# A long causal convolution: the layout in DRAM of a tile's rows, and the transfers that read four shifted copies of it back

## The chip, the cores and the metric

One core of one Trainium2 chip runs the whole program in one launch. The metric is the time of one execution on the device, in microseconds (us); the kernel before takes 1078.66 us in the median of three runs. Names of engines: PE is TensorE (matmuls), DVE is VectorE, ACT is ScalarE, POOL is GpSimd, SP is SyncE, which here only issues transfers.

## The reference

A small model in float32 on 256 positions of width 1024: a block with sliding-window attention and an mLSTM, cross attention, a gated feed-forward; then a conformer convolution module, a second feed-forward, a sparse attention, a third feed-forward. The change touches the convolution module alone, which is:

```
def conformer_conv_module(h, w_in, b_in, w_dw, b_dw, ln_g, ln_b, w_out):
    a, g = jnp.split(h @ w_in + b_in, 2, axis=-1)
    u = a * jax.nn.sigmoid(g)
    u = lax.conv_general_dilated(
        u, w_dw[:, None, :].astype(u.dtype), window_strides=(1,),
        padding=[(CONV_WIDTH - 1, 0)], dimension_numbers=('NWC', 'WIO', 'NWC'),
        feature_group_count=D_MODEL) + b_dw
    ...
    uf = (uf - mu) * lax.rsqrt(var + LN_EPS) * ln_g.astype(jnp.float32) + ln_b.astype(jnp.float32)
    u = jax.nn.silu(uf).astype(h.dtype)
    return u @ w_out
```

`CONV_WIDTH` is 31 and the convolution is depthwise: each of the 1024 channels has 31 taps of its own over time, and sees only earlier positions. `mu` and `var` are mean and variance over the channels of one position.

## The kernel before

Activations lie with channels on the 128 partitions and time along the row: a tensor of 1024 channels is 8 tiles m = 0 to 7 of 128 x 256. Weights stream from DRAM in 512 KB pieces (`wraw`, issued by SP, four buffers) and most are split by ACT and DVE into a high and a low half (`wpr`), so that three fast matmuls make one float32 product (L260 to L262).

The convolution module is the function `conformer`. For each tile m it has these steps, named as in the code:

- `p` (PE, L1120): the product with `w_in`; `g`, `h` (DVE, ACT): scaling and the gate; `u` (DVE, L1143): the gated tile, written into `uz`, where 19 zero columns stand before its 256 columns. A row of `uz` has ZW = 275 numbers, 1100 bytes.
- `w` (POOL, L1150): a transfer of the tile to DRAM, into one of five buffers `cz`, row p of the tile as row p of the buffer.
- `c` (POOL, L1158): four transfers back into SBUF, into one of five buffers `crp`. Copy s (0 to 3) is shifted by s columns and goes to partitions 32 s to 32 s + 31; on partition 32 s + c lie the channels c, 32 + c, 64 + c and 96 + c, each as a piece of 272 numbers (1088 bytes). For tiles 5 to 7 the step first loads the tile's tap weights (`cwd`, L1077), which for tiles 0 to 4 are loaded at the stage's start.
- `t` (PE, L1167): 16 or 20 tap matmuls (the profile counts each of them twice). Since a partition group holds the same 32 channels at four shifts, one matmul with a sparse weight of 128 x 32 does four taps of 32 channels. The first 16 or 20 of the 31 taps of a tile are done so.
- `d`, `v`, `n`, `y` (DVE, ACT, L1197 and near): the other taps, one multiply-add over the tile each; `m` (DVE, L1210): the sum of both parts; `q`, `s` (ACT, PE, L1243): sums for the layer norm. After tile 7's sums come mean, variance and the product with `w_out` (steps `sf` to `o`), one after the other.

The order of the steps on each engine is worked out when the program is built. `Plan.run` simulates the engines with the time that each step is given (`step(name, engine, us, need, rank, lag=...)`: `us` is how long it holds its engine, `lag` how much later its result is there) and issues the steps in the order of their planned starts. Each engine then works its queue strictly in that order; what really releases a step are semaphores. A transfer issued by POOL signals one of eight semaphores in turn, and an issue waits until the transfer eight places before has landed. POOL has little other work in this stage than `w`, `c` and the loads of taps. In the profile a transfer issued by POOL shows as POOL's instruction DMA_DIRECT2D for its issue; its landing is told by "DMA cz<-cuz" or "DMA crp<-cz" as the releaser of a wait.

Of the kernel before, what the change touches and what calls it, by code (L numbers as in the profile page):

```python
# [132 lines left out]
class Net:  # L133
# [919 lines left out]
    def conformer(self, first, pool):  # L1053
        nc = self.nc
        W = 31
        PAD = 4 * max(CONV_G) - 4
        ZW = PAD + 3 + S
        NREP = 5
        uz = pool.tile([P, KT, ZW], F32, name="cuz")
# [3 lines left out]
        zs = [dram.tile([P, ZW], F32, name=f"cz{i}")[:, :] for i in range(NREP)]  # L1063
# [11 lines left out]
        def taps_of(m):  # L1075
            wd[m] = pool.tile([P, max(CONV_G), P], F32, name="cwd", tag="cwd", bufs=NREP)
            nc.gpsimd.dma_start(wd[m][:, 0 : CONV_G[m]], self.T["c_dw"][:, m, 0 : CONV_G[m], :])  # L1077
# [18 lines left out]
        def step(name, eng, us, need=(), rank=0, **kw):  # L1096
            return lambda fn: plan.add(name, eng, us, fn, need, rank, **kw)

        @step("r", "pe", 0.6, at=5.5, lag=0.5)
        def _():  # L1100
            got["rb"] = self.bcast(r12, "x")
# [6 lines left out]
        for m in range(KT):  # L1108
# [36 lines left out]

            @step(f"w{m}", "gp", 0.6, [f"u{m}"] + ([f"c{m - NREP}"] if m >= NREP else []), 0, lag=2.5)
            def _(m=m):
                nc.gpsimd.dma_start(zs[m % NREP], uz[:, m, :])  # L1150

            @step(f"c{m}", "gp", 2.3 if m < NREP else 2.9, [f"w{m}"] + ([f"t{m - NREP}"] if m >= NREP else []), 0, lag=3.5)
            def _(m=m):
                if m >= NREP:
                    taps_of(m)
                z, r = zs[m % NREP], reps[m % NREP]
                for s in range(4):
                    nc.gpsimd.dma_start(r[32 * s : 32 * s + 32, :, 0 : ZW - 3],  # L1158
                                        bass.AP(tensor=z.tensor, offset=s, ap=[[ZW, 32], [32 * ZW, 4], [1, ZW - 3]]))

            @step(f"t{m}", "pe", 0.03 + 0.48 * CONV_G[m], [f"c{m}"] + ([f"m{m - 3}"] if m >= 3 else []), 2 if m else 0)
            def _(m=m):
# [727 lines left out]
```

## Time and profile before

| | |
|---|---|
| median of 3 runs | 1078.66 us (1078.24 to 1082.45) |
| the profiled execution | 1083.75 us, its span 1082.0 us |
| mean granted clock of TensorE | 0.990 of full speed |
| POOL, busy | 127.5 us, 335 instructions |
| transfers issued by POOL (q0) | 2560 packets, 7.95 MB, 2.8% of 16 DMA engines' span |
| transfers issued by SP (q1) | 52056 packets, 170.14 MB, 49.5% |
| `crp<-cz`, the reads | 32, 136.0 KB each, 4.0 us in the median from issue to landing |
| `cz<-cuz`, the writes | 8, 137.5 KB each, 5.2 us |
| where the transfers lie in the span | first write issued at 449.55 us, last reads from 502.97 to 505.18 |

The span is the time from the first to the last instruction; the profiled execution is a little longer than its span, and differs from the median since it is one run. Busy is time in which an engine worked; an idle engine matters only where the chain that ended last goes through it. Sizes in KB are of 1024 bytes in the list of issues. The rows that the argument rests on stand in a section of their own below.

### The profile page before, as it was taken

How to read it: one execution, taken by the hardware profiler on the slowest of the kernel's cores; microseconds unless marked ns; L12 is line 12 of the kernel's file. 1: busy time of each engine (PE TensorE's matmuls, PEld its weight loads, DVE VectorE, ACT ScalarE, POOL GpSimd, SP SyncE). 2: the span in 40 equal slices, each digit the busy share in tenths (PEclk: the TensorE clock that was granted, in tenths of full speed). 3: DMA queues.
4: the chain of work that ended last, by engine and by line, in shares of the span. 5: the costliest groups of instructions: out<-in, count | busy, mean ns of one | idle time of the engine just before them, and what ended most of it. 6: DMA issues, size and time to landing. Idle time of an engine off the chain costs nothing.

```text
span 1082.0 us, 19870 instructions
## 1 busy us (share of the span) xinstructions
PE 1062.6 (98%) x7550; PEld 973.2 (90%) x7550; DVE 786.7 (73%) x1645; ACT 604.2 (56%) x1134; POOL 127.5 (12%) x335
## 2 busy tenths in 40 slices
PE   9999999999999999998999999999999999999998
PEld 8999999999999988984988888889998998888887
DVE  5886667757888865687988778665668657777763
ACT  7675556556666644422766666444466755666530
POOL 1020003002000000334030000013332112000000
PEclk8999999999999999998999999999999999999999
DMA  8654444434555665486555556655073035556670
GB/s 260 214 168 144 143 132 156 156 118 157 194 195 185 206 182 171 145 213 178 186 190 187 189 185 211 191 183 160 27 223 109 2 118 173 185 190 188 184 210 20
DMA packets 54711, 179.34 MB, mean 166 GB/s; under 512 B 9176, under 2 KB 11096, under 8 KB 54616
## 3 DMA queue, kind: packets, MB, share of 16 engines
q1 hardware_dynamic: 52056, 170.14, 49.5%
q0 software_dynamic: 2560, 7.95, 2.8%
q8 instruction: 59, 0.97, 0.4%
q14 instruction: 36, 0.29, 0.1%
HBM read 175.88 MB, written 2.17 MB: 165 GB/s over the span
## 4 chain that ended last, share of the span: by engine, by line
PE 84%; DVE 5%; DMA 5%; POOL 2%; ACT 2%; issue 2%; SPq 0%; ACTq 0%; POOLq 0%
PE pb L268 29%; PE pb L269 15%; PE pb L260 10%; PE pb L261 10%; PE pb L262 10%; DMA cz<-cuz 3%; POOL crp L1158 1%; DVE wpr L233 1%; DVE xx L410 1%; ACT wpr L232 1%; PE bh L1494 1%; DVE xres L527 1%; PE bt L1167 1%; PE pb L317 1%; DMA wraw<-in_n_out_dram 1%
## 5 line engine op out<-in xcount | busy, mean ns | idle before, releaser
L233 DVE TENSOR_TENSOR wpr<-wraw,wpr 128x1024 fp32r<-128x1024 f32 (+1 forms) x300 | 361.4, 1208 | 161.3 <-ACT wpr L232 159.0
L232 ACT CAST wpr<-wraw 128x1024 fp32r<-128x1024 f32 (+1 forms) x300 | 309.3, 1034 | 190.9 <-PE pb L269 98.0
L268 PE MATMUL pb<-xx,wpr 128*128 128x512 f32 x840 | 294.1, 393 | 0.0
L269 PE MATMUL pb<-xx,wpr 128*128 128x256 f32 x840 | 235.4, 280 | 0.0
L268 PEld LDWEIGHTS pb<-xx,wpr 128*128 128x128 f32 x840 | 158.4, 189 | 33.9
L268 PE MATMUL pb<-fhs,wpr 128*128 128x512 f32 x528 | 186.0, 394 | 0.0
L269 PEld LDWEIGHTS pb<-xx,wpr 128*128 128x128 f32 x840 | 158.5, 189 | 0.0
L269 PE MATMUL pb<-fhs,wpr 128*128 128x256 f32 x528 | 147.3, 279 | 0.0
L260 PE MATMUL pb<-xx,wpr 128*128 128x256 f32 x456 | 130.8, 288 | 0.0
L261 PE MATMUL pb<-xx,wpr 128*128 128x256 f32 x456 | 130.2, 286 | 0.0
L262 PE MATMUL pb<-xx,wpr 128*128 128x256 f32 x456 | 129.3, 284 | 0.0
L268 PEld LDWEIGHTS pb<-fhs,wpr 128*128 128x128 f32 x528 | 99.0, 187 | 23.1
L269 PEld LDWEIGHTS pb<-fhs,wpr 128*128 128x128 f32 x528 | 99.0, 187 | 0.0
L260 PEld LDWEIGHTS pb<-xx,wpr 128*128 128x128 f32 x456 | 87.4, 192 | 1.4
L261 PEld LDWEIGHTS pb<-xx,wpr 128*128 128x128 f32 x456 | 87.8, 193 | 0.9
L262 PEld LDWEIGHTS pb<-xx,wpr 128*128 128x128 f32 x456 | 87.7, 192 | 0.0
L260 PE MATMUL pb<-yy,wpr 128*128 128x256 f32 x256 | 72.8, 284 | 0.7 <-ACT yy L1306 0.7
L261 PE MATMUL pb<-yy,wpr 128*128 128x256 f32 x256 | 71.9, 281 | 0.4 <-DVE yy L1310 0.4
L262 PE MATMUL pb<-yy,wpr 128*128 128x256 f32 x256 | 71.8, 281 | 0.0
L992 ACT COPY ft<-pb 128x256 f32<-128x256 f32 x105 | 38.7, 369 | 54.9 <-PE pb L269 54.9
L260 PE MATMUL pb<-wpr,xx 128*128 128x256 f32 x176 | 50.4, 286 | 0.0
L261 PE MATMUL pb<-wpr,xx 128*128 128x256 f32 x176 | 49.8, 283 | 0.0
(442 smaller groups left out, 1954.7 us busy)
## 6 DMA issues: line engine op xcount, KB each, us to landing
wraw<-in_up_dram SPq DMA_DIRECT2D x44, 512.0 KB, 4.4
wraw<-in_up2a_dram SPq DMA_DIRECT2D x44, 512.0 KB, 4.4
wraw<-in_up2b_dram SPq DMA_DIRECT2D x44, 512.0 KB, 4.1
wraw<-in_w_in_dram SPq DMA_DIRECT2D x22, 512.0 KB, 4.8
wraw<-in_n_in_dram SPq DMA_DIRECT2D x20, 512.0 KB, 4.2
wraw<-in_wkv_dram SPq DMA_DIRECT2D x16, 512.0 KB, 4.5
wraw<-in_dn_dram SPq DMA_DIRECT2D x16, 512.0 KB, 4.3
wraw<-in_c_in_dram SPq DMA_DIRECT2D x16, 512.0 KB, 4.3
```

The costliest lines, as they stand in the source:

```text
L232: self.nc.scalar.copy(both[:, 0, :], raw)
L233: return lambda: self.nc.vector.tensor_tensor(both[:, 1, :], raw, both[:, 0, :].bitcast(F32), op=ALU.subtract)
L260: mm(out, left[:, 0], right[:, 0], start=start, stop=False, skip_group_check=True)
L261: mm(out, left[:, 0], right[:, 1], start=False, stop=False, skip_group_check=True)
L262: mm(out, left[:, 1], right[:, 0], start=False, stop=stop, skip_group_check=True)
L268: mm(out, left[:, 0], right, start=start, stop=False, skip_group_check=True)
L269: mm(out[:, 0], left[:, 1], right[:, 0], start=False, stop=stop, skip_group_check=True)
L317: mm(b[i][:, 0:S], w[k][:, lo, i * P : i * P + P], self.xx[:, k, ro], start=(k == 0 and lo + ro == 0), stop=(k == KT - 1 and lo == 1), ski ...
L410: nc.vector.scalar_tensor_tensor(lo, src, g, hi.bitcast(F32), op0=ALU.mult, op1=ALU.subtract)
L527: self.nc.vector.tensor_tensor(self.x[:, m, :], acc[m // 2][:, (m % 2) * S : (m % 2) * S + S], self.x[:, m, :], op=ALU.add)
L992: nc.scalar.copy(t, b[:, 1])
L1158: nc.gpsimd.dma_start(r[32 * s : 32 * s + 32, :, 0 : ZW - 3], bass.AP(tensor=z.tensor, offset=s, ap=[[ZW, 32], [32 * ZW, 4], [1, ZW - 3]]))
```

## The change

The buffer in DRAM holds the tile in another order, and the reads become one. Channel 32 j + c of the tile, which stood in row 32 j + c of the buffer, goes to row 4 c + j: the four channels that share a partition of the copies are neighbours, a run of 4 x 275 = 1100 numbers (4400 bytes). The write's pattern in DRAM is (4 steps of ZW) x (32 steps of 4 ZW) x (ZW numbers), from the same 128 rows of SBUF. Copy s on partition 32 s + c is then one run of 4 x 275 - 3 = 1097 numbers (4388 bytes) from place 4 ZW c + s, so one transfer with the pattern (4 steps of 1) x (32 steps of 4 ZW) x (1097 numbers) fills all 128 partitions. The last three columns of each piece of 275 are those of the next channel and are not used by the matmuls. In the plan the step `c` gets 0.6 us instead of 2.3 (1.2 instead of 2.9 with the load of taps) and a lag of 5.2 us instead of 3.5, the same sum.

```diff
@@ -1145,18 +1145,20 @@
             @step(f"w{m}", "gp", 0.6, [f"u{m}"] + ([f"c{m - NREP}"] if m >= NREP else []), 0, lag=2.5)
             def _(m=m):
-                nc.gpsimd.dma_start(zs[m % NREP], uz[:, m, :])
-
-            @step(f"c{m}", "gp", 2.3 if m < NREP else 2.9, [f"w{m}"] + ([f"t{m - NREP}"] if m >= NREP else []), 0, lag=3.5)
+                z = zs[m % NREP]
+                nc.gpsimd.dma_start(bass.AP(tensor=z.tensor, offset=0, ap=[[ZW, 4], [4 * ZW, 32], [1, ZW]]), uz[:, m, :])
+
+            @step(f"c{m}", "gp", 0.6 if m < NREP else 1.2, [f"w{m}"] + ([f"t{m - NREP}"] if m >= NREP else []), 0, lag=5.2)
             def _(m=m):
                 if m >= NREP:
                     taps_of(m)
                 z, r = zs[m % NREP], reps[m % NREP]
-                for s in range(4):
-                    nc.gpsimd.dma_start(r[32 * s : 32 * s + 32, :, 0 : ZW - 3],
-                                        bass.AP(tensor=z.tensor, offset=s, ap=[[ZW, 32], [32 * ZW, 4], [1, ZW - 3]]))
+                n = 4 * ZW - 3
+                nc.gpsimd.dma_start(r.rearrange("p j t -> p (j t)")[:, 0:n],
+                                    bass.AP(tensor=z.tensor, offset=0, ap=[[1, 4], [4 * ZW, 32], [1, n]]))
```

The instructions of PE, DVE, ACT and SP stand in the same order before and after, apart from line numbers (lines below the edit move by 2). On POOL the first tiles stood like this; `cz0` to `cz4` and `crp0` to `crp4` are the five buffers on each side, and x4 are the four reads of one tile:

```order
L1150 DMA cz0_5183<-cuz_5179 128x275
L1150 DMA cz1_5184<-cuz_5179 128x275
L1158 DMA crp0_5207<-cz0_5183 32x4x272 x4
L1158 DMA crp1_5208<-cz1_5184 32x4x272 x4
L1150 DMA cz2_5185<-cuz_5179 128x275
L1158 DMA crp2_5209<-cz2_5185 32x4x272 x4
```

Between the write of tile 1 and that of tile 2 stood eight issues. Now, at the same place of POOL's queue:

```order
L1152 DMA cz0_5183<-cuz_5179 4x32x275
L1152 DMA cz1_5184<-cuz_5179 4x32x275
L1160 DMA crp0_5207<-cz0_5183 128x1x1097
L1160 DMA crp1_5208<-cz1_5184 128x1x1097
L1152 DMA cz2_5185<-cuz_5179 4x32x275
L1160 DMA crp2_5209<-cz2_5185 128x1x1097
```

The places of the writes and reads are the same, with two issues between the writes of tiles 1 and 2. The end of the stage on POOL, tiles 5 to 7 (buffers 0 to 2 again, `cwd` is the load of a tile's taps), stood like this:

```order
L1150 DMA cz0_5183<-cuz_5179 128x275
L1077 DMA cwd_5606<-in_c_dw_dram 128x640
L1158 DMA crp0_5207<-cz0_5183 32x4x272 x4
L1150 DMA cz1_5184<-cuz_5179 128x275
L1077 DMA cwd_5713<-in_c_dw_dram 128x640
L1158 DMA crp1_5208<-cz1_5184 32x4x272 x4
L1150 DMA cz2_5185<-cuz_5179 128x275
L1077 DMA cwd_5790<-in_c_dw_dram 128x640
L1158 DMA crp2_5209<-cz2_5185 32x4x272 x4
```

Each read waits for the write two places before it. With the change:

```order
L1152 DMA cz0_5183<-cuz_5179 4x32x275
L1077 DMA cwd_5591<-in_c_dw_dram 128x640
L1160 DMA crp0_5207<-cz0_5183 128x1x1097
L1152 DMA cz1_5184<-cuz_5179 4x32x275
L1077 DMA cwd_5695<-in_c_dw_dram 128x640
L1160 DMA crp1_5208<-cz1_5184 128x1x1097
L1152 DMA cz2_5185<-cuz_5179 4x32x275
L1077 DMA cwd_5762<-in_c_dw_dram 128x640
L1160 DMA crp2_5209<-cz2_5185 128x1x1097
```

The order is the same, with one read for four in each tile.

## Rows read from the trace of the kernel before

**Rows 1.** The page's busy time (us), share of the span and instructions of TensorE.

```profile
PE 1062.6 (98%) x7550; PEld 973.2 (90%) x7550; DVE 786.7 (73%) x1645; ACT 604.2 (56%) x1134; POOL 127.5 (12%) x335
```

**Rows 2.** The page's chain that ended last, share of the span by line.

```profile
PE pb L268 29%; PE pb L269 15%; PE pb L260 10%; PE pb L261 10%; PE pb L262 10%; DMA cz<-cuz 3%; POOL crp L1158 1%; DVE wpr L233 1%; DVE xx L410 1%; ACT wpr L232 1%; PE bh L1494 1%; DVE xres L527 1%; PE bt L1167 1%; PE pb L317 1%; DMA wraw<-in_n_out_dram 1%
```

**Rows 3.** Waits between 440 and 520 us: us in total, times, longest.

```profile
POOL crp L1158 <- DMA cz<-cuz: 31.7, 7, 6.9
...
DVE cy L1210 <- PE bt L1167: 6.4, 2, 5.3
...
PE bt L1167 <- DMA crp<-cz: 4.0, 2, 3.3
```

**Rows 4.** Timeline of PE: start us, us, line, count [idle before <- releaser].

```profile
463.96 1.93 PE L1167 MATMUL bt<-crp,cwd 128*32 128x256 f32 x32
...
480.63 7.07 PE L1120 MATMUL pb<-cxg,wraw 128*128 128x256 f32 x32
487.64 5.39 PE L1167 MATMUL bt<-crp,cwd 128*32 128x256 f32 x96
...
496.71 2.37 PE L1167 MATMUL bt<-crp,cwd 128*32 128x256 f32 x40 [0.67 <-DMA crp<-cz]
502.38 4.50 PE L1167 MATMUL bt<-crp,cwd 128*32 128x256 f32 x40 [3.30 <-DMA crp<-cz]
...
507.73 2.52 PE L1167 MATMUL bt<-crp,cwd 128*32 128x256 f32 x40
```

**Rows 5.** Timeline of DVE, same columns.

```profile
454.36 0.42 DVE L1143 SCALAR_TENSOR_TENSOR cuz<-cag 128x256 f32<-128x256 f32 x1
...
490.09 0.41 DVE L1143 SCALAR_TENSOR_TENSOR cuz<-cag 128x256 f32<-128x256 f32 x1
...
501.19 0.45 DVE L1197 SCALAR_TENSOR_TENSOR cy<-cuz,par,cy 128x231 f32<-128x231 f32 x1
506.93 0.42 DVE L1210 TENSOR_TENSOR cy<-bt,cy 128x256 f32<-128x256 f32 x1 [5.29 <-PE bt L1167]
...
510.31 0.42 DVE L1210 TENSOR_TENSOR cy<-bt,cy 128x256 f32<-128x256 f32 x1 [1.15 <-PE bt L1167]
```

**Rows 6.** Chain that ended last, in time order: shortest, longest later write.

```profile
459.76 3.62 DMA cz<-cuz
...
475.02 7.14 DMA cz<-cuz
```

**Rows 7.** Timeline of POOL, columns as for PE.

```profile
455.38 4.39 POOL L1158 DMA_DIRECT2D crp<-cz  x8 [4.49 <-DMA cz<-cuz]
...
499.42 0.56 POOL L1150 DMA_DIRECT2D cz<-cuz  x1
...
502.97 2.21 POOL L1158 DMA_DIRECT2D crp<-cz  x4 [2.43 <-DMA cz<-cuz]
```

**Rows 8.** Line 1158 from 502.9 us: c7's reads (ns) and landing.

```profile
L1158 POOL DMA_DIRECT2D crp<-cz x4: 552/558/569, 503.0 to 504.6; - x4
...
DMA to landing us min/median/max: 2.9/2.9/3.0
```

**Rows 9.** DMA issues between 440 and 512 us: count, KB, median us to landing.

```profile
wraw<-in_c_in_dram SPq DMA_DIRECT2D x6, 512.0 KB, 7.4
wraw<-in_c_out_dram SPq DMA_DIRECT2D x6, 512.0 KB, 4.5
```

**Rows 10.** Stretches: us, busy per engine (instructions), PE clock, DMA share, GB/s.

```profile
449.00:451.00 2.00, 2.00 (x20) 2.00 (x19) 1.63 (x5) 2.00 (x6) 1.15 (x2) 1.00 0.96 318
458.00:460.00 2.00, 2.00 (x11) 1.74 (x11) 2.00 (x6) 0.91 (x2) 2.00 (x5) 1.00 1.00 230
466.00:468.00 2.00, 2.00 (x10) 1.77 (x11) 2.00 (x7) 1.00 (x3) 0.66 (x2) 1.00 0.91 244
498.80:500.00 1.20, 0.28 (x8) 0.00 (x0) 1.20 (x4) 0.17 (x1) 1.20 (x4) 1.00 0.83 225
502.40:507.70 5.30, 5.30 (x48) 2.44 (x49) 0.77 (x3) 0.31 (x1) 4.00 (x13) 0.50 0.48 129
```
## Prediction

> **What bounds the kernel now.** I read the share of busy time first: TensorE (PE) is busy 98% of the span [rows 1], so a change on the DMA side can only win where PE stands still or runs slowly. The chain of work that ended last says where the changed lines count: the landing of the DRAM writes (`cz<-cuz`) holds 3% of the whole span and the issuing of the reads (L1158) 1% [rows 2]. All of it lies in the conformer stage, 440 to 520 us. There the waits read: the queue of GpSimd (POOL) stood 31.7 us before reads, waiting for a write to land; VectorE (DVE) stood 6.4 us for the tap matmuls; PE itself stood only 4.0 us for a read [rows 3]. So 40 us of chain shrink to a few us of lost PE and DVE time, and these lie at the end of the stage. I call the steps by the names in the code: u (DVE makes the gated tile), w (write to DRAM), c (read of four shifted copies), t (tap matmuls), m (DVE adds t).
>
> PE works without a hole through p7 and t1 to t3 (from 487.64). Then t6 starts only at 502.38, after 3.30 us of waiting for c6, and takes 4.50 us for 40 matmuls; t7 starts at 507.73 and takes 2.52 [rows 4]. The granted clock between 502.4 and 507.7 was 0.50, the lower of TensorE's two levels, after PE had stood idle; in the stretches before it is 1.00 [rows 10]. DVE ends its last tap at 501.64 (501.19 + 0.45), waits 5.29 us for t6, does m6 at 506.93 and m7 at 510.31 [rows 5]. What follows m7 (the layer-norm sums) is a serial chain that moves with it.
>
> Why c7 is late: u7 is ready at 490.50 (490.09 + 0.41) [rows 5], but w7 is issued at 499.42 [rows 7], 8.9 us later. POOL's queue is in order, and it stands w, c, w, c: each w stands behind four reads, which wait for the write before. One turn is a write's latency (3.6 to 7.1 us for w2 to w6, of which the shortest and the longest stand in [rows 6]), 0.28 us to the next issue and 2.2 us for four issues [rows 7].
>
> **The change part by part.** *Issues.* Four reads of 0.55 us become one. I take the same 0.55 us for the new one, since reads of 128 pieces and writes of 128 rows show 0.55 and 0.56 here [rows 7, 8]. Per tile POOL saves 3 x 0.55 = 1.65 us. PE, DVE, ScalarE and SyncE keep their order; on POOL too the w and c steps keep theirs.
>
> *The first two tiles.* Between c0's start at 455.38 and w2 stand eight issues, 4.39 us [rows 7]; now two, 1.1 us. u2 is ready at 454.78 [rows 5], so w2 goes out 3.3 us earlier, at 456.5 instead of 459.76. No other wait takes this place: the only thing w2 waits for beyond u2 is an early load.
>
> *The five turns from c2 to c7.* Each is shorter by 1.65 us if issuing sets it, and by nothing if bytes do, for the write stands in the same queue behind the reads, and the bytes stay the same: 4 x 128 x 1088 = 557 KB before, 128 x 4388 = 562 KB after. The rows say bytes: between 458 and 460, and 466 and 468, the DMA engines are 100% and 91% busy at 230 and 244 GB/s [rows 10]. Longer rows should help a little: with rows of 2 to 4 KB the engines moved 318 GB/s at a share of 0.96, with the 1.1 KB pieces of c6 alone 225 GB/s at 0.83 [rows 10]. Per engine that is 318/(16 x 0.96) = 20.7 and 225/(16 x 0.83) = 16.9 GB/s, so 562 KB take 1.7 us with all engines instead of 2.1. I take 0.2 us a turn, 1 us for five; the ends are 0 and 8.25, but w7 cannot go before u7, which caps the sum with the 3.3 us at 8.6.
>
> *c7 itself.* Its four reads took from 502.97 to 504.6 + 3.0 = 507.6, 4.6 us [rows 7, 8]. One transfer of 562 KB: the nearest rows are the loads of 512 KB in 128 rows of 4 KB, with a median of 4.5 us for those of `c_out`, in and after the end of the stage, and of 7.4 for those of `c_in`, where loads and reads overlap [rows 9]. Nothing but one tap load stands beside c7, so I take 4.5. The Trainium skill (DMA: Bandwidth & Descriptors, "Anatomy of one DMA") gives 2.0 us plus bytes over 436 GB/s for a transfer issued by GpSimd, an estimate of 3.3 us here; the 512 KB rows are longer than that and I go by them; by the rule c7 would land 1.2 us sooner.
>
> *The write.* Same 128 rows of 1100 B, scattered to a pitch of 4400 B instead of one run. Nearest row: the old write, 3.6 us at its shortest in the chain [rows 6]. Below, nothing; above, see the second rival. I take no change.
>
> *Sum.* c7 is issued at 502.97 - 3.3 - 1.0 = 498.7 and lands at 503.2. c6 is issued a turn before c7, at least 4.4 us (0.28 + 0.55 + 3.6), and lands by 498.8; so t6 follows t5, which ends at 499.08, without a hole, takes t5's 2.37 us instead of 4.50 [rows 4], and m6 no longer waits. t7 starts at 503.2, ends at 505.6, and m7 starts then instead of at 510.31: 4.7 us won. If c7 lands by 501.3, DVE becomes the limit: from m6 to m7 it had 510.31 - 1.15 idle - 506.93 = 2.2 us of work (m6, a tap, a weight split, an add) [rows 5], so m7 cannot start before 501.64 + 2.2 = 503.9, and at most 6.4 us are won. If the turns save nothing and c7 takes its old 4.6 us, c7 lands at 504.3 and 3.6 us are won. One more stop: c6's tap load reuses t1's buffer, and t1 ends near 489.4 (a third of 5.39 us after 487.64 [rows 4]); c6 cannot pass 490, which costs nothing at this forecast.
>
> The profiled execution took 1083.75 us around its span of 1082.0; the median of the runs is 1078.66. 1083.75 - 4.7 = 1079.05, a ratio of 0.99566; times 1078.66 this is **1074.0 us**. Its own range is 1072.3 (6.4 won) to 1075.1 (3.6 won).
>
> **The rivals.**
> *One: bytes set every turn, and the early w2 is eaten too.* For it: 91 to 100% busy DMA engines from 458 on, and that a write's latency grew to 7.14 us where loads overlap [rows 6, 10]. Against it: in the end stretch the engines are at 48% [rows 10], and 225 GB/s is no ceiling when 318 was seen. c7 then lands at 506 to 507.6, 0 to 2 us are won: 1077.7 us.
>
> *Two: four DMA engines instead of sixteen, each transfer on others.* Both new patterns in DRAM begin with a dimension of 4, where the old ones began with 128 and 32. Should the transfer be dealt out by it, four engines at 20.7 GB/s each carry it: the read takes 562/83 = 6.8 us of transfer instead of 1.8 (562/318), so 4.5 + 5.0 = 9.5 us to land; the write 141/83 = 1.7 instead of 0.4, so 4.9. Writes then go beside reads, the turns are short, w7 goes at 490.8, c7 at 496.0, lands at 505.5, m7 stands at 507.9: 2.4 us won. But c0, sent at 455.38 + 1.3, lands at 466.2, and PE wants it at 463.96 [rows 4]: 2.2 us lost ahead of everything. Net 0.2 us: 1078.5 us, from 1075.5 to 1081. No row before has an outermost dimension below 32 on this queue, so the trace neither bears it out nor denies it. The Trainium skill (DMA: Bandwidth & Descriptors, "Why a DMA increments its semaphore by 16 and not by 1") states such a rule: the number of engines is the largest up to 16 that divides the slowest dimension of both sides, with consecutive engines from a moving cursor; it also says that some direct copies issued by GpSimd keep 16. By that rule this rival decides.
>
> *Three, slower: the same four engines each time.* Every tile then puts 703 KB on four engines, 703/83 = 8.5 us, reads and writes in one line, with the weight loads sharing them. Eight tiles from 456.7 end at 524.7, at the least 17 us after 507.6: 1096 us. It decides from the point where a tile's transfer is longer than one p step of PE, 7.1 us [rows 4]. A milder form is rival two with slower engines, for instance at the 14.4 GB/s that 230 GB/s over 16 engines at 100% make: the read takes 9.8 us of transfer and 12.5 to land, c0 lands at 469.2, PE loses 5.2 us at t0, w7 (5.6 us) goes at 496.0, c7 at 501.9 and lands at 514.4, m7 stands at 516.8: 6.5 us lost, 1085 us.
>
> **How the numbers follow.** Forecast 0.42, rival one 0.14, rival two 0.25, rival three with its milder form 0.19. A measurement here can tell about 0.5% from no change, 5.4 us: faster by more needs 1073.3 or less, 5.4 us won, the upper third of the forecast's range; since 0.2 us a turn is a cautious take I give it 0.21 of the 0.42, and 0.03 of rival two: 0.24. Slower by more is rival three and 0.01 of rival two's bad side: 0.20. Within 0.5%: 0.56. The range goes from 1072.0 (DVE's limit and a little) to 1083 (rival two's bad side and the edge of the milder form of three); about 0.16 lie above, 0.03 below.
>
> **What would show it.** Right: POOL's reads are eight issues of 0.55 us; w2 goes at about 456.5; c7's latency is 4 to 5 us; PE's hole before t6 is gone, the clock stays at 1.00 through 502 to 508, and m7 starts 4 to 6 us earlier against p7's end. Wrong: the wait of POOL for writes stays near 31 us with w7 still at 499 (rival one); the reads land 8 to 11 us after issue, with low GB/s at a low share of busy engines, and PE waits at t0 (rival two); w lands later than its reads and each turn exceeds 8 us (rival three).

## The result and the profile after

The changed kernel takes 1117.31 us in the median of three runs (1117.2 to 1125.91) against 1078.66 before: 1.036 times the time, 95% interval 1.0323 to 1.0397. It is slower; forecast were 1074.0 us and a range from 1072.0 to 1083. The profiled execution of after took 1117.2 us, its span 1115.4. The loss lies in the conformer stage: from the issue of w0 to the start of m7 it was 449.55 to 510.31 before [rows 5], 60.8 us, and is 444.80 to 542.23 now, 97.4 us, 36.7 more. Ahead of the stage, where nothing was changed, this run was 4.75 us faster than the profiled one of before, and behind it 1.5 us slower, so the spans differ by 33.4 us.

The page: the share of PE has fallen from 98% [rows 1] to 96%, and POOL's queue (q0) moves the same 8.0 MB in 6016 packets instead of 2560.

```profile
PE 1067.0 (96%) x7550; PEld 973.3 (87%) x7550; DVE 787.1 (71%) x1645; ACT 604.1 (54%) x1134; POOL 114.1 (10%) x311
...
q0 software_dynamic: 6016, 8.01, 2.9%
```

The waits of the stage, 440 to 560 us (us in total, times, longest), beside [rows 3]: POOL waits 69.8 us for writes instead of 31.7, and PE 32.9 us for reads instead of 4.0.

```profile
POOL crp L1160 <- DMA cz<-cuz: 69.8, 7, 14.6
...
DVE cy L1212 <- PE bt L1169: 40.6, 5, 10.3
...
PE bt L1169 <- DMA crp<-cz: 32.9, 5, 8.1
```

POOL's timeline (start us, us, line, count, idle before and its releaser), to be held against [rows 7]:

```profile
450.37 0.69 POOL L1160 DMA_DIRECT2D crp<-cz  x1 [4.04 <-DMA cz<-cuz]
451.51 0.69 POOL L1160 DMA_DIRECT2D crp<-cz  x1 [0.45 <-issue]
452.19 0.71 POOL L1152 DMA_DIRECT2D cz<-cuz  x1
467.49 0.67 POOL L1160 DMA_DIRECT2D crp<-cz  x1 [14.59 <-DMA cz<-cuz]
...
515.41 0.70 POOL L1160 DMA_DIRECT2D crp<-cz  x1 [9.60 <-DMA cz<-cuz]
516.11 0.71 POOL L1152 DMA_DIRECT2D cz<-cuz  x1
...
527.28 0.70 POOL L1160 DMA_DIRECT2D crp<-cz  x1 [9.90 <-DMA cz<-cuz]
```

w2 goes out at 452.19, 2.2 us after u2 (450.0) instead of 5.0: the forecast's second step came true. But it lands at 467.2, and c2 waits 14.59 us for it. From c2 to c7 it is 59.8 us for five turns, 12.0 each; before it was 463.92 to 502.97, 7.8 each ([rows 7] has c7; c2 was the line below).

```profile
463.92 2.19 POOL L1158 DMA_DIRECT2D crp<-cz  x4 [3.60 <-DMA cz<-cuz]
```

The chain that ended last, in time order (start us, us, what), shows what a turn is made of:

```profile
504.54 10.59 DMA cz<-cuz
515.13 0.28 issue
515.41 0.46 POOL crp L1160
515.87 0.24 issue
516.11 10.89 DMA cz<-cuz
527.00 0.28 issue
527.28 10.53 DMA crp<-cz
537.81 0.14 issue
537.95 4.26 PE bt L1169 x40
```

A write of 141 KB takes 10.59 and 10.89 us to land where the shortest took 3.62 [rows 6], and c7 takes 10.53 where its four parts took 4.6 [rows 7, 8]. PE stands for it at t0, which the forecast had at no cost, and at t4 to t7:

```profile
464.45 3.64 PE L1169 MATMUL bt<-crp,cwd 128*32 128x256 f32 x32 [5.16 <-DMA crp<-cz]
...
503.47 4.39 PE L1169 MATMUL bt<-crp,cwd 128*32 128x256 f32 x40 [6.82 <-DMA crp<-cz]
...
515.09 3.71 PE L1169 MATMUL bt<-crp,cwd 128*32 128x256 f32 x40 [6.80 <-DMA crp<-cz]
526.92 4.50 PE L1169 MATMUL bt<-crp,cwd 128*32 128x256 f32 x40 [8.12 <-DMA crp<-cz]
...
537.95 4.22 PE L1169 MATMUL bt<-crp,cwd 128*32 128x256 f32 x40 [5.99 <-DMA crp<-cz]
```

After each hole the 40 matmuls take 3.7 to 4.5 us instead of 2.4, for the granted clock is near its lower level: 0.61 in the mean from 510 to 530. The same view (us, busy per engine, clock, DMA share, GB/s) shows the transfers: 69 GB/s at a share of 0.29 from 521 to 526, while little but the rows of one read moves. That is about four of sixteen engines busy (16 x 0.29 = 4.6), and 17 GB/s for each of four.

```profile
510.00:530.00 20.00, 6.79 (x72) 3.55 (x76) 3.14 (x9) 0.42 (x1) 4.03 (x12) 0.61 0.31 75
521.00:526.00 5.00, 0.00 (x0) 0.00 (x0) 0.13 (x1) 0.00 (x0) 0.00 (x0) 0.53 0.29 69
```

### The profile page after: what moved, and what is told of

Same layout as the page of the kernel before. It is cut to its first block, busy times and chain, and to the rows that moved or that the text cites. A ratio compares the mean times of both kernels' runs of the same rounds, so it can differ in the third digit from the quotient of the medians.

```text
span 1115.4 us, 19829 instructions
## 1 busy us (share of the span) xinstructions
PE 1067.0 (96%) x7550; PEld 973.3 (87%) x7550; DVE 787.1 (71%) x1645; ACT 604.1 (54%) x1134; POOL 114.1 (10%) x311
## 3 DMA queue, kind: packets, MB, share of 16 engines
q0 software_dynamic: 6016, 8.01, 2.9%
## 4 chain that ended last, share of the span: by engine, by line
PE 78%; DMA 7%; issue 5%; DVE 5%; ACT 4%; POOL 1%; SPq 0%; ACTq 0%; POOLq 0%
PE pb L268 27%; PE pb L269 14%; PE pb L260 9%; PE pb L261 9%; PE pb L262 9%; DMA cz<-cuz 3%; ACT wpr L232 1%; DVE wpr L233 1%; DMA crp<-cz 1%; DMA wraw<-in_n_in_dram 1%; PE bh L1496 1%; DVE xx L410 1%; DMA xres<-in_x_dram 1%; DVE xres L527 1%; PE bs L1594 1%
## 5 line engine op out<-in xcount | busy, mean ns | idle before, releaser
L1169 PE MATMUL bt<-crp,cwd 128*32 128x256 f32 x288 | 25.8, 530 | 32.9 <-DMA crp<-cz 32.9
L1169 PEld LDWEIGHTS bt<-crp,cwd 128*32 128x32 f32 x288 | 12.6, 147 | 44.8 <-issue 37.2
```

The lines of the kernel that those rows point to most:

```text
L1169: nc.tensor.matmul(bt[m][c, 0:S], wd[m][:, i, c], reps[m % NREP][:, j, PAD - 4 * i : PAD - 4 * i + S], start=(i == 0), stop=(i == CONV_G[m ...
```

## Theories and experiments

Two theories together, called A and C in the expectations. A: a transfer whose outermost dimension is 4 is carried by four DMA engines. C: a write's landing comes only after the reads issued ahead of it, even when its own bytes are long done. B and D in the expectations are rivals, and each says there what it means. Rivals: the 4.4 KB rows or the 4400-byte pitch are slow in themselves; the write is slow because its own rows go to four engines. Each run is compared with the kernel before on the same chip (there 1080.5 to 1082.4 us in the median). The diffs below are cut to the transfers; the times that the plan gives to the steps w and c were set to match, without changing their sums.

The trace of after bears on both theories by itself. A transfer from POOL raises its semaphore sixteen times, and the trace records when. Of c7, issued at 527.28, twelve of these signals come 1.8 to 2.9 us after the issue and the last four at 8.9 to 10.5 us; in the packet records its rows of 4388 bytes move four at a time from 529.2 to 535.2. That is theory A. Of w6, issued at 516.11 behind c6, all 32 packets of 4400 bytes are through by 520.30. Twelve of its signals have come by 521.0, and the last four come between 525.9 and 527.0, some 0.2 us behind the last four of c6 (525.7 to 526.8). That is theory C, on POOL's queue: the bytes are done 6.7 us before the landing.

**The same long rows in four reads.** Undoes the outermost 4 of the read alone:

```diff
-                nc.gpsimd.dma_start(r.rearrange("p j t -> p (j t)")[:, 0:n],
-                                    bass.AP(tensor=z.tensor, offset=0, ap=[[1, 4], [4 * ZW, 32], [1, n]]))
+                for s in range(4):
+                    nc.gpsimd.dma_start(r.rearrange("p j t -> p (j t)")[32 * s : 32 * s + 32, 0:n],
+                                        bass.AP(tensor=z.tensor, offset=s, ap=[[4 * ZW, 32], [1, n]]))
```

> The changed layout and the changed write, but the 4.4 KB rows read by four transfers, one per shift, each with an outermost dimension of 32 (plan times of the step c as before). Theory A (a transfer is dealt to DMA engines by the outermost dimension of its pattern in DRAM; 4 gives four engines): each read lands 3 to 7 us after issue, as in the kernel before; only the write is slow; 1078 to 1088 us. Theory B (long rows, unaligned and four times over the same bytes, are slow to read): four reads of a tile together still take 9 us or more, POOL waits on; 1105 us or more.

1085.01 us, ratio 1.0027 (1.0012 to 1.0043). The time lies in the range of theory A. c7's four reads land in 2.7 to 3.0 us each again, so the rows of 4388 bytes are not what is slow. The write, still with outermost 4, lands in 5.2 us in the median, as before the change: behind short reads its four engines cost little (4.6 us at the shortest, before 3.3; 8.6 at the longest, before 7.1).

**The old write, stated as 4 x 32 rows.**

```diff
-                nc.gpsimd.dma_start(zs[m % NREP], uz[:, m, :])
+                nc.gpsimd.dma_start(bass.AP(tensor=z.tensor, offset=0, ap=[[32 * ZW, 4], [ZW, 32], [1, ZW]]), uz[:, m, :])
```

> The kernel before, layout, rows and reads untouched; only the write's pattern in DRAM is stated as 4 x 32 x 275 instead of 128 x 275, the same addresses in the same order. Theory A: the write runs on four engines, its transfer takes about 1.7 us instead of 0.4, each turn of POOL's queue up to 1.3 us more; 1079 to 1088 us, with the last write landing 4 to 5 us after issue instead of 3.3. Theory B (only the long rows are slow): no change, 1077 to 1082 us, 3.3 us.

1080.84 us, ratio 0.9983 (0.9964 to 1.0002). It tells nothing of the theories: the trace has the write of before, issued in 0.56 us (0.71 in the change), and 2560 packets on q0. The 128 rows lie one behind another in DRAM, so the statement was probably folded back to 128 x 275 when the program was built.

**One read, outermost 32.** One transfer as in the change; the copies lie on partition 4 c + s, with the rows of the tap weights reordered to match. Of the changed line the pattern alone is shown.

```diff
-ap=[[1, 4], [4 * ZW, 32], [1, n]]
+ap=[[4 * ZW, 32], [1, 4], [1, n]]
```

> The changed kernel with the same layout, the same write, the same single read of 128 rows of 4388 B, but the copies lie on partition 4 c + s instead of 32 s + c (tap weights reordered likewise in the weight layout), so the read's pattern starts with 32 instead of 4. Theory A: sixteen engines, the read lands in 4 to 8 us, w7 close behind u7; 1073 to 1081 us. Theory B (long rows or overlapping rows are slow): as the changed kernel, 1105 to 1118 us.

1081.08 us, ratio 0.9992 (0.9979 to 1.0005). The same bytes in one issue, the two outer dimensions swapped: the whole loss comes back. It does not go below that, as theory A's range (to 1081) allowed: the writes, still with outermost 4, land in 6.8 us in the median (5.2 before), and w7 goes out 6.7 us after u7, not close behind it. The reads' landings (line 1160: us, minimum, median, maximum), first after, then this kernel:

```profile
DMA to landing us min/median/max: 9.7/11.4/14.4
```

```profile
DMA to landing us min/median/max: 3.6/5.3/6.7
```

The packets show the engines. In the window of c7 q0 had (packets, MB, share of 16 engines) in after and in this kernel:

```profile
q0 software_dynamic: 528, 0.56, 20.8%
```

```profile
q0 software_dynamic: 144, 0.56, 45.4%
```

In the packet records 128 of each are the rows of 4388 bytes, the others are of 4 bytes: 16 here, 400 in after. 400 is 16 and 12 x 32: as if each of twelve engines without rows got as many fillers as a loaded one gets rows. With outermost 32 some 14 to 17 rows move at a time (four in after), and the sixteen signals of c7 all come 3.1 to 3.9 us after its issue.

**Two reads, each with outermost 4.** As many bytes, in two issues of 64 rows in place of the one read; the tap weights' rows are reordered to match.

```diff
+                for h in range(2):
+                    nc.gpsimd.dma_start(r.rearrange("p j t -> p (j t)")[64 * h : 64 * h + 64, 0:n],
+                                        bass.AP(tensor=z.tensor, offset=64 * ZW * h, ap=[[1, 4], [4 * ZW, 16], [1, n]]))
```

> The changed kernel with its one read cut into two of 64 rows of 4388 bytes, each still with an outermost dimension of 4 (copies on partition 64 h + 16 s + c', the tap weights' rows reordered to match); same bytes, same row size, one issue more. If each transfer goes to four engines and the next one to others, eight engines now carry a tile: 16 rows of 236 ns on each engine are 3.8 us instead of 7.6, c7 lands 6 to 7.5 us after its first issue instead of 10.5, each turn falls by 3 to 4 us from 11.3, six turns and c7 give back 18 to 28 us of the 35 lost: 1087 to 1100 us. If both go to the same four engines, c7 still takes 10 to 11.5 us and the time is 1113 to 1122. If long rows with an outermost dimension of 4 were slow for another reason than the number of engines (the start of the transfer, say), two issues make it worse: above 1120.

1102.78 us, ratio 1.0197 (1.0153 to 1.0242): nearly half of the loss comes back, somewhat less than expected. c7's second half lands 9.1 us after the first issue (10.5 in after); in the records the rows move eight at a time only from 520.8 to 523.2, since the second half starts some 1.5 us after the first, and a row takes 290 ns instead of 236. So the next transfer does go to other engines (four at a time before and after that), and the number of engines sets the time of a read.

**Only the write on sixteen engines** (four of 32 rows, outermost 32, in place of the one write; the read as in the change).

```diff
+                for j in range(4):
+                    nc.gpsimd.dma_start(bass.AP(tensor=z.tensor, offset=j * ZW, ap=[[4 * ZW, 32], [1, ZW]]), uz[32 * j : 32 * j + 32, m, :])
```

> The changed kernel with its read unchanged (outermost 4), the write alone as four of 32 rows. Theory C (on this queue a write's landing comes only after the read issued ahead of it, since all engines report in the queue's order): the writes still land 9 to 11 us after issue, each turn is 11 to 13 us, POOL waits 60 us or more for writes, and the time stays at 1113 to 1122 us. Rival B (the write is slow because its own rows go to four engines): the writes land in 4 to 5 us, turns are about 7 us, and the time falls to 1080 to 1092.

1122.47 us, ratio 1.0378 (1.035 to 1.0406): nothing comes back, at the upper edge of what theory C expected. The chain shows the last of a tile's four writes, on all engines:

```profile
482.83 11.42 DMA cz<-cuz
...
497.01 9.14 DMA cz<-cuz
...
508.88 9.05 DMA cz<-cuz
```

The read issued just ahead of each tile's writes lands at 492.99, 505.42 and 517.06, and the first write 0.16 to 0.22 us behind it. Of the signals of the writes behind these last two reads twelve come by 1.8 us after the issue and the last four with those of the read. Theory C holds; a write's own engines don't matter behind such a read.

**The change, its write issued by ScalarE.**

```diff
-            @step(f"w{m}", "gp", 0.6, [f"u{m}"] + ([f"c{m - NREP}"] if m >= NREP else []), 0, lag=2.5)
+            @step(f"w{m}", "ac", 0.1, [f"u{m}"] + ([f"c{m - NREP}"] if m >= NREP else []), 0, lag=3.0)
...
-                nc.gpsimd.dma_start(bass.AP(
+                nc.scalar.dma_start(bass.AP(
```

> The changed kernel with the writes issued from ScalarE's queue instead of GpSimd's, everything else the same (ScalarE's order gets eight issues more). Theory C (a transfer from GpSimd's queue counts as landed only when all sixteen engines have reported, so a write behind a read waits for the whole read though its own four engines are done): writes land 3 to 5 us after issue beside the reads, POOL's turns shrink, the reads keep 9 to 13 us; 1083 to 1098 us. Theory D (write and read share the same four engines and stand in one line there): writes still land with the reads; 1110 us or more.

1095.55 us, ratio 1.0116 (1.0101 to 1.0131). Two thirds of the loss come back. The trace has w going out as soon as u is ready, and several reads in flight at once. But the writes land 3.6 to 17.4 us after their issue, not in the 3 to 5 us that theory C expected, and the reads in 11.3 to 19.3 us, not 9 to 13. The chain has the slowest write, w5:

```profile
478.28 17.40 DMA cz<-cuz
495.68 0.02 issue
```

c4, issued on POOL at 473.86, landed at 493.20, the load of taps behind it at 494.94, and w5 right after these, 17.40 us after its issue. That is not theory C over two queues. In the packet records the 128 rows of w5 (1100 bytes each, on ScalarE's own queue) move only from 484.55 to 494.48, so here the bytes stood in line, more as theory D has it; on which engines, the records do not tell. Nor does the order of issue hold over the queues: w4, issued at 469.71, landed at 473.34, ahead of c2, issued at 466.28 and landed at 477.56. A write with outermost 4 from ScalarE raises its semaphore five times in the trace, not sixteen (w5: once 1.0 us after its issue, four times from 16.2 to 17.4 us).

**Sixteen engines on both sides**, all from POOL: the read with outermost 32 and the four writes, both as shown above, five issues a tile as before.

> The changed layout with the read stated with an outermost dimension of 32 (copies on partition 4 c + s, the tap weights' rows reordered to match) and the write as four of 32 rows, also outermost 32. If only the number of DMA engines made the change slow, then with sixteen on both sides a write lands 3.5 to 7 us after its last issue, as before; POOL has five issues a tile, as before, so the time is that of the kernel before: 1077 to 1083 us, ratio 0.995 to 1.001, and POOL's longest wait for a write is below 8 us. If the write's pitch of 4400 bytes in DRAM is slow in itself, the writes still land 8 to 11 us after issue and the time is 1090 or more.

1078.68 us, ratio 0.9972 (0.9956 to 0.9988). The writes land in 5.2 us in the median, as before, and POOL's longest wait for one is 5.7 us. The pitch is harmless, and the layout without the outermost 4 takes 2.9 us less than the kernel before on the same chip.

**The read with outermost 32, the plain write from ScalarE**, both edits as shown above.

> The read with outermost 32 (sixteen engines) as in the run of that read alone, and the write (outermost 4) issued from ScalarE's queue instead of POOL's, so that it no longer stands behind the reads. Theory C: the write lands in 3 to 5 us whatever reads are in flight, POOL's queue holds only reads, c7 is issued by 497 us and the end of the stage is bound by DVE: 1071 to 1077 us, ratio 0.990 to 0.996. Rival (bytes: the engines are full with the weight loads, so that the order of transfers decides nothing): 1079 to 1083.

1078.32 us, ratio 0.9957 (0.9936 to 0.9978), the upper end of the ratio that C expected, and a time between the two ranges. w7 goes out with u7 at 490.42 but lands 7.95 us later, since its rows move only from 493.49 to 497.94; c7 is issued at 498.89, not by 497.

**The kernel before, its write from ScalarE.** The old layout and four short reads; only the step `w` changes, as above.

> The kernel before, with its write issued from ScalarE's queue instead of POOL's; the four short reads stay. If what the end of the stage waits for is the one queue in which writes stand behind reads, this alone gives back what the forecast hoped for: 1072 to 1077 us, ratio 0.991 to 0.996. If the number of issues on POOL or the bytes set the turns, it stays within 1078 to 1083.

> The same kernel as the one before with its writes issued from ScalarE's queue, timed again in more rounds: if its gain is real, the ratio is 0.990 to 0.994 again; if it was the luck of four runs, it is 0.997 or more.

1073.67 us, ratio 0.9924 (0.9903 to 0.9945); again, in more rounds, 1074.30 us and 0.9943 (0.9923 to 0.9963), a little less of a gain but far from 0.997. This is the version that beats both. Its chain from w7 to m7:

```profile
486.88 4.81 DMA cz<-cuz
...
492.54 1.35 POOL crp L1158 x3
...
494.17 3.73 DMA crp<-cz
497.90 0.14 issue
498.04 2.40 PE bt L1167 x40
500.44 0.02 issue
500.46 0.43 DVE cy L1210
```

w7 goes out 0.03 us after u7 instead of 8.9, PE keeps its clock (1.00 granted from 498.0 to 500.5; 2.40 us for 40 matmuls), and from w0 to m7 it is 54.8 us instead of 60.8. The landings of its writes are as before (1.9, 5.0 and 7.1 us: minimum, median, maximum; before 3.3, 5.2, 7.1): what is won is the moment of issue.

**One read with outermost 32, four writes from ScalarE**, the edits as shown above, with `nc.scalar` for `nc.gpsimd` in the four writes.

> Sixteen engines on both sides (one read with outermost 32, four writes of 32 rows) and the writes from ScalarE's queue. If four engines for the write are what the run with the read alone and ScalarE's write lost against the kernel before with ScalarE's write (ratios 0.9957 and 0.9924), then the single read now costs nothing against the four short ones: ratio 0.989 to 0.993, 1070 to 1074 us. If instead the one read of 4.4 KB rows is no better than four short ones and four issues on ScalarE (about 0.33 us each by the run with ScalarE's plain write) hold up its gate steps, the ratio is 0.994 to 0.998.

1079.34 us, ratio 0.998 (0.9963 to 0.9997), the upper end of the second expectation. The four writes of tile 1 hold ScalarE for 3.82 us, u2 is 9.5 us behind u1 instead of 4.7, and most of the gain is gone: that reading rests on this one trace.

## Why the prediction was wrong, point by point

- *What bounds the kernel* was right: w7 stands behind POOL's queue, and m7 hangs on it. Taking w out of that queue wins 5.9 us of the stage, close under the cap of 6.4 that the forecast worked out from DVE.
- *Issues*: one read costs 0.69 us (0.67 to 0.70), not 0.55; still 1.5 us a tile saved. A small miss.
- *The first two tiles*: right as far as it goes, w2 left 2.2 us after u2; but w2 then took 15.0 us to land.
- *The five turns*, 0.2 us each won: measured 4.2 us each lost. The reason given was wrong too: the reads of before were no 1.1 KB pieces on the wire. In the window of c7 before (502.9 to 508 us) q0 has 128 packets of 4352 bytes, four pieces in each, as many as the change has rows; the other three above 2 KB, of 5120 bytes, are the end of a load of taps.

```profile
DMA packets 201, 0.57 MB, mean 112 GB/s; under 512 B 70, under 2 KB 70, under 8 KB 201
```

- *c7 itself*, 4.5 us: this is the step that failed first. Its nearest rows, the loads of 512 KB, run on sixteen engines; with outermost 4 it measured 10.53, with outermost 32 3.88 in one issue. Rival two had 9.5, for the right reason: four engines, and the next transfer on others. The Trainium skill (DMA: Bandwidth & Descriptors, "Why a DMA increments its semaphore by 16 and not by 1") has the rule that the slowest dimensions set the number of engines; the traces agree with it, four rows at a time and 69 GB/s at a share of 0.29, and the exception for some direct copies did not apply here.
- *The write*, no change: measured 10.7 us in the median (5.3 to 15.0) instead of 5.2, the step that cost most, and it failed in rival two as well ("writes then go beside reads"). Their bytes do go beside them (those of w6 were through by 520.30), but from POOL they land after them (w6 at 527.00). The Trainium skill (DMA: Bandwidth & Descriptors, "Queues, rings and completion order") says that the increment of the semaphore lands only after every earlier write of that engine, across its queues; its section "Why a DMA increments its semaphore by 16 and not by 1" says that all sixteen report for a transfer that GpSimd issues. By these two every landing from POOL waits for the four loaded engines; the sixteen signals of w6, and the 9.0 to 11.4 us of writes on sixteen engines, agree with that. That it holds between two queues no run here shows: the 17.40 us of a write from ScalarE were its bytes. None of this was weighed in the forecast.
- *Rival three* came nearest in time (1096) by a mechanism that did not happen: c0 and c1 ran on different engines, together (of c1's last eight signals four come just behind the last of c0, at 464.4 to 464.5, and four from 465.3 to 465.9). The line in which all stand is that of the landings; a turn is a read (11.2 us from issue to landing in the mean of c2 to c6) plus 0.7 us around it, 12.0 us, and not 8.5 us of bytes.
- *The sum*: the 36.7 us of the stage can be read off POOL's queue. From w0 to c2 it is 8.3 us more (444.80 to 467.49, before 449.55 to 463.92), since w2 goes out earlier but lands later. The five turns from c2 to c7 are 20.7 us more. From c7's issue to m7 it is 7.6 us more: c7 with 5.9 and t7, at the lower clock, with 1.7 (4.22 us instead of 2.52). PE's wait of 5.16 us at t0 is not on this path: no later write waits for it.

## What to carry to other kernels

Before merging transfers, look at the outermost dimension of the merged pattern: swapping two dimensions of the pattern in DRAM made 3.7% of the time here (ratios 1.036 and 0.9992), at the same bytes, rows and number of issues. Before hoping for longer rows, look at the packets that the short ones already become. A transfer on the critical chain is helped by going out early: from POOL it lands only after what was issued there ahead of it, and beside reads on four engines another queue alone did not make its landing short (up to 17.40 us).

## What the runs showed of the hardware that was not expected

- Where every transfer signals sixteen times, landings follow the order of issue nearly without exception: of the pairs issued from 440 us on in the stage that overlapped, 2 of 58 landed the other way round in after, and 3 of 240 in the kernel before with its write from ScalarE. In the change with its write issued by ScalarE, five signals each, it is 15 of 116. Weight loads on SP's queue are held too: one issued at 457.59, behind c0 and c1, took 9.3 us, one at 474.50 3.9 us; whether its bytes or its signals were late is not told apart.
- POOL's write of 128 rows of 1100 bytes moves as 32 packets of 4400 bytes, before the change and after; the same write from ScalarE moves as 128 packets of 1100.
- A transfer with outermost 4 costs POOL 0.69 us to issue instead of 0.55, and some 384 packets of 4 bytes more.
- A write issued by ScalarE holds that engine 0.33 us when its 128 rows lie one behind another in DRAM, and 0.5 us with outermost 4 (the first one 1.1 us).
